# Layer 1's down projection in a two-layer trunk: seven block products in place of eight

## The chip, the cores and the metric

The kernel runs on one core of a Trainium2 chip. The metric is the device time of one execution, in microseconds (us). The engines are TensorE (PE in the profile; its weight loads are PEld), VectorE (DVE), ScalarE (ACT), GpSimd (POOL) and SyncE (SP). SP issues the loads from device memory; GpSimd's queue issues a few transfers within the core that add what they read onto what is there.

## The reference

A decoder trunk of two layers on 512 tokens of width 1024, float32 throughout. Each layer has a mixer (convolution and pooling in layer 0, chunked spatial gating in layer 1) and then a gated FFN with a causal convolution of width 3; a final RMS norm ends it. The change lies in layer 1's FFN:

```python
def gated_conv_ffn(x, w_gate, w_up, conv_w, conv_b, w_down):   # x: (1, 512, 1024)
    g = jnp.einsum('bsd,df->bsf', x, w_gate)                    # d_ff = 2816
    g = causal_dwconv3(g, conv_w) + conv_b
    up = jnp.einsum('bsd,df->bsf', x, w_up)
    return jnp.einsum('bsf,fd->bsd', jax.nn.silu(g) * up, w_down)

for layer in range(2):
    ...
    h = h + gated_conv_ffn(rms_norm(h, norm_ffn[layer]), ...)
return rms_norm(h, final_norm)
```

## The kernel before

**Splits.** Every float32 matrix is kept as two parts in the type float32r: hi is a rounded copy, lo is what is left. A product of two matrices is three matmuls (hi hi, hi lo, lo hi; lines 133 to 135). hi is made on ScalarE (`nc.scalar.activation(hi, raw, AF.Copy)`), lo on VectorE by a subtraction (`parts`, L126 to L130; `split` for activations, L247 and L249). A second way, `summed`, makes lo without VectorE: ScalarE writes the negative of the hi part, and a transfer on GpSimd's queue adds the source to it (L120, L121).

**Seven products.** Some hidden products (gate and up projections) already work on 2 x 2 blocks with seven products instead of eight (Winograd's form of Strassen's scheme), from sums of weight blocks and of activation blocks. For these `both` (gate and up) and `seven` (up alone, with plain gate products) treat a pair of FFN tiles f, f+1. An FFN tile is 128 of the 2816 hidden channels; there are 22. Products that share an accumulator share a PSUM bank: products 1, 6, 7 and 4 bank a, 5 and 3 bank e, 2 bank b.

**FFN 1.** `PARTS` says which pairs are made before which down group: (0, 2) then tiles 0 and 1; (4) then 2 to 5; (6, 8) then 6 to 9; (10, 12) then 10 to 13; (14, 16) then 14 to 17; (18, 20) then 18 to 21. So one period of the steady part is a pair by `both`, a pair by `seven`, and a down group. At the end of a pair the gate goes through the convolution (`conv`, c in a pool of two buffers) and the silu (`silu`, one s tile of 128 x 512 per FFN tile, three buffers), is multiplied by the up projection, and is split by `act` into a_hi and a_lo (four buffers each in layer 1 too).

**The down group.** For four tiles `group8` fetches four weight rows of 128 x 1024 (`raw_dn`), splits them with `parts` into whi_dn and wlo_dn, and makes eight outputs (four token tiles by two column halves) in eight PSUM banks, with the activations stationary and the weights moving. Its order is output by output, four tiles each, and a finished output is added to y on VectorE:

```python
dst = y[t][:, half * 512 : (half + 1) * 512]
nc.vector.tensor_tensor(dst, ps, dst, ALU.add)
```

The last group also squares, scales and stores the outputs.

**Order.** The framework's scheduler orders each engine's queue from the program; it may put later, ready work ahead. `inorder` (`tc.keep_in_program_order`) fixes the order among the instructions so marked. Each engine then works through its queue in order, so an instruction that waits holds up all behind it. Buffers are pools with a fixed count: four for fetched weights (`raw`, 512 KB each), six each for whi and wlo, three for weight sums (`sum`), seven PSUM banks and one more. A fetch waits until the last reader of its buffer is done, a transfer among them.

Of the kernel before, what the change touches and what calls it, by code (L numbers as in the profile page):

```python
# [30 lines left out]
def tile_trunk(ctx: ExitStack, tc: tile.TileContext, x, norm_mix, norm_ffn, final_norm,  # L31
# [3 lines left out]
    nc = tc.nc  # L35
    x = x[0]
# [4 lines left out]
    tp = ctx.enter_context(tc.tile_pool(name="tp", bufs=2))  # L41
# [3 lines left out]
    def mm_bank(name):  # L45
        return ps_mm.tile([P, 512], F32, tag="mm", name=name)
# [28 lines left out]
    inorder = tc.keep_in_program_order  # L75
# [49 lines left out]
    def parts(raw, a, b, name):  # L125
        hi = wp.tile([P, a, b], F32R, tag="whi", bufs=6, name=f"whi_{name}")  # L126
        lo = wp.tile([P, a, b], F32R, tag="wlo", bufs=6, name=f"wlo_{name}")
        nc.scalar.activation(hi, raw, AF.Copy)  # L128
        nc.vector.tensor_tensor(lo, raw, hi.bitcast(F32), ALU.subtract)  # L129
        return hi, lo  # L130
# [113 lines left out]
    def split(pool, src, name, scale=1.0, tag="a", bufs=None):  # L244
        hi = pool.tile([P, S], F32R, tag=f"{tag}hi", bufs=bufs, name=f"{name}_hi")
        lo = pool.tile([P, S], F32R, tag=f"{tag}lo", bufs=bufs, name=f"{name}_lo")
        nc.scalar.activation(hi, src, AF.Copy, scale=scale)  # L247
        if isinstance(scale, float):
            nc.vector.tensor_tensor(lo, src, hi.bitcast(F32), ALU.subtract)  # L249
# [227 lines left out]
    HALF = S // 2  # L477
# [10 lines left out]
    class Ffn:  # L488
# [5 lines left out]

        def __init__(self, layer, prm, norm, ap, sums):
            self.layer, self.prm, self.ap, self.acts = layer, prm, ap, {}
            self.norm, self.sums = norm, sums
            self.t23, self.t41 = {}, {}  # L500

        def conv(self, t, ft):
            ap, prm, n = self.ap, self.prm, f"{self.layer}_{ft}"
            c = ap.tile([P, S], F32, tag="c", bufs=2, name=f"c{n}")
            nc.scalar.activation(c, t[:, 0:S], AF.Copy, scale=prm("cf", ft))
            for i in (1, 2):
                nc.vector.scalar_tensor_tensor(c, t[:, i : S + i], prm("cf", i * NF + ft), c,  # L507
                                               op0=ALU.mult, op1=ALU.add)
# [102 lines left out]
        def multiply(self, banks, name, product, weights_):  # L611

            at = self.BANK[product]
            first = at not in banks
            if first:
                banks[at] = mm_bank(f"{name}{at}")
            ps = banks[at][:, :HALF]
            hi, lo = weights_
            for kp in range(NP):
                b_hi, b_lo = self.moving(product, kp)  # L620
                a_hi, a_lo = hi[:, kp, :], lo[:, kp, :]
                for l, r, end in ((a_hi, b_hi, False), (a_hi, b_lo, False),
                                  (a_lo, b_hi, kp == NP - 1)):
                    nc.tensor.matmul(ps, l, r, start=first, stop=end, skip_group_check=True)
                    first = False
            return ps
# [333 lines left out]
    def ffn1(norm):  # L960
        with tc.tile_pool(name="f1", bufs=1) as ap:
            def sums(kp):
                return [cp.tile([P, 2, HALF], F32R, tag=f"h{k}", name=f"t23_{k}")
                        for k in (kp, kp + NP)]

            ffn = Ffn(1, prm1, norm, ap, sums)
            acts = ffn.acts
            y = [ap.tile([P, D], F32, name=f"y{t}") for t in range(NT)]
            ssf = ap.tile([P, NT, PAD], F32, name="ssf")[:, :, :2]

            def turn_residual(t, half):
                ps = mm_bank(f"hT{t}_{half}")
                for i in range(4):
                    nc.tensor.transpose(ps[:, i * P : (i + 1) * P],
                                        h[half * 4 + i][:, t * P : (t + 1) * P], ident)
                nc.scalar.copy(y[t][:, half * 512 : (half + 1) * 512], ps)

            def before(i, j):
                if i < 2:
                    turn_residual(j, i)  # L980

            for groups, a, b in PARTS:
# [13 lines left out]

                def lhs(ft, j):
                    ts_ = slice((j // 2) * P, (j // 2 + 1) * P)
                    return acts[ft][0][:, ts_], acts[ft][1][:, ts_]

                def rhs(ft, j):
                    c = slice((j % 2) * 512, (j % 2 + 1) * 512)
                    return ch[ft][0][:, 0, c], ch[ft][1][:, 0, c]

                yf = {}

                def done(j, ps):
                    t, half = j // 2, j % 2
                    dst = y[t][:, half * 512 : (half + 1) * 512]
                    nc.vector.tensor_tensor(dst, ps, dst, ALU.add)  # L1010
# [5 lines left out]
                    yf[half] = ap.tile([P, S], F32, tag="s", bufs=3, name=f"yf{j}")  # L1016
                    nc.vector.tensor_tensor(yf[half], dst, fin[:, half * 512 : (half + 1) * 512],
                                            ALU.mult)
                    if half == 0:
                        nc.vector.tensor_scalar(ss, ss, 1.0 / D, EPS, op0=ALU.mult, op1=ALU.add)  # L1020
                        return
                    ms = ssf[:, t, 0:1]
                    nc.vector.scalar_tensor_tensor(ms, ss, 1.0 / D, ms, op0=ALU.mult, op1=ALU.add)
                    r = tp.tile([P, LINE], F32, tag="rc", name=f"rc_fin{t}")[:, :1]
                    newton(ms, 1, f"fin{t}", r)
                    nc.vector.tensor_scalar(ms, ms, 1.5, None, op0=ALU.add)
                    for c in range(2):
                        cs = slice(c * 512, (c + 1) * 512)
                        nc.vector.tensor_scalar(y[t][:, cs], yf[c], r, ms,
                                                op0=ALU.mult, op1=ALU.mult)  # L1030
# [16 lines left out]
    n = mixer0()  # L1047
# [33 lines left out]
```

## Time and profile before

| | |
|---|---|
| device time, median of 3 runs | 1006.06 us (1005.46 to 1007.25) |
| span of the profiled execution, first to last instruction | 1004.4 us |
| TensorE busy | 992.1 us, 99% of the span |
| VectorE, ScalarE, GpSimd busy | 666.0, 499.9, 94.1 us |
| layer 1's down matmuls | 528 of 128x512 |
| granted TensorE clock, mean | 0.999 |

In the profile's rows, a line such as L1010 is a line of the kernel; then come engine, operation, the tiles written and read (buffer numbers left out) and the shape. A group's row ends with its count, total and mean time. In a timeline a row starts with the start and the duration in us; in square brackets stands how long the engine was idle before it, and what ended that. A window's row gives for each engine its busy us and, in brackets, its number of instructions. TensorE's matmuls overlap, so the mean duration of one (0.39 us for 128x512) is longer than the step from one to the next.

### The profile page before, as it was taken

How to read it: one execution, taken by the hardware profiler on the slowest of the kernel's cores; microseconds unless marked ns; L12 is line 12 of the kernel's file. 1: busy time of each engine (PE TensorE's matmuls, PEld its weight loads, DVE VectorE, ACT ScalarE, POOL GpSimd, SP SyncE). 2: the span in 40 equal slices, each digit the busy share in tenths (PEclk: the TensorE clock that was granted, in tenths of full speed). 3: DMA queues.
4: the chain of work that ended last, by engine and by line, in shares of the span. 5: the costliest groups of instructions: out<-in, count | busy, mean ns of one | idle time of the engine just before them, and what ended most of it. 6: DMA issues, size and time to landing. Idle time of an engine off the chain costs nothing.

```text
span 1004.4 us, 14019 instructions
## 1 busy us (share of the span) xinstructions
PE 992.1 (99%) x5547; PEld 865.9 (86%) x5547; DVE 666.0 (66%) x993; ACT 499.9 (50%) x735; POOL 94.1 (9%) x109
## 2 busy tenths in 40 slices
PE   8999999999999999999999999999999999999997
PEld 6888888898989989899878888888989898898985
DVE  5977457968584775847833645389675857658567
ACT  6523345754553635537645434675535365353553
POOL 3032030200000000000300001212000000000000
PEclk9999999999999999999999999999999999999999
DMA  7532234554445444454433123435545345353432
GB/s 236 178 105 84 85 90 122 117 155 114 118 142 131 128 110 119 138 137 127 127 125 104 63 85 105 101 88 123 150 100 153 105 127 147 94 152 112 127 85 84
DMA packets 80749, 120.30 MB, mean 120 GB/s; under 512 B 4164, under 2 KB 53548, under 8 KB 80684
## 3 DMA queue, kind: packets, MB, share of 16 engines
q1 hardware_dynamic: 73580, 98.96, 30.9%
q0 software_dynamic: 5760, 18.88, 10.7%
q10 hardware_dynamic: 1344, 1.58, 0.5%
q8 instruction: 43, 0.70, 0.3%
q14 instruction: 22, 0.18, 0.1%
HBM read 98.42 MB, written 2.10 MB: 100 GB/s over the span
## 4 chain that ended last, share of the span: by engine, by line
PE 95%; DMA 2%; DVE 2%; ACT 1%; SPq 0%; issue 0%; POOL 0%; DVEq 0%; ACTq 0%; POOLq 0%
PE dn L133 4%; PE dn L135 4%; PE dn L134 4%; PE d L133 4%; PE d L134 4%; PE d L135 4%; PE gu L133 3%; PE g L133 3%; PE g L134 3%; PE gu L134 3%; PE gu L135 3%; PE g L135 3%; PE u L135 1%; PE oo L133 1%; PE oo L135 1%; PE u L134 1%
## 5 line engine op out<-in xcount | busy, mean ns | idle before, releaser
L507 DVE SCALAR_TENSOR_TENSOR c<-rows,prm,c 128x512 f32<-128x512 f32 x88 | 68.9, 792 | 0.3
L134 PE MATMUL d<-a_lo,whi_d 128*128 128x512 f32 x176 | 68.6, 390 | 0.0
L135 PE MATMUL d<-a_hi,wlo_d 128*128 128x512 f32 x176 | 68.5, 389 | 0.0
L133 PE MATMUL dn<-whi_dn,a_hi 128*128 128x512 f32 x176 | 68.4, 390 | 0.0
L134 PE MATMUL dn<-wlo_dn,a_hi 128*128 128x512 f32 x176 | 68.4, 390 | 0.0
L135 PE MATMUL dn<-whi_dn,a_lo 128*128 128x512 f32 x176 | 67.6, 390 | 0.0
L133 PE MATMUL d<-a_hi,whi_d 128*128 128x512 f32 x176 | 67.1, 390 | 0.0
L1010 DVE TENSOR_TENSOR y<-dn,y 128x512 f32<-128x512 f32 x48 | 32.3, 688 | 30.9 <-PE dn L135 30.7
L133 PE MATMUL g<-hgh,whi_g 128*128 128x512 f32 x128 | 50.0, 391 | 0.0
L134 PE MATMUL g<-hgl,whi_g 128*128 128x512 f32 x128 | 50.0, 391 | 0.0
L135 PE MATMUL g<-hgh,wlo_g 128*128 128x512 f32 x128 | 49.8, 389 | 0.0
L129 DVE TENSOR_TENSOR wlo_dn<-raw_dn,whi_dn 128x1024 fp32r<-128x1024 f32 x22 | 26.8, 1222 | 30.7 <-ACT whi_dn L128 30.7
L129 DVE TENSOR_TENSOR wlo_d<-raw_d,whi_d 128x1024 fp32r<-128x1024 f32 x22 | 26.8, 1221 | 30.2 <-ACT whi_d L128 30.2
L129 DVE TENSOR_TENSOR wlo_u<-raw_u,whi_u 128x1024 fp32r<-128x1024 f32 x16 | 19.6, 1223 | 34.2 <-ACT whi_u L128 34.1
L120 ACT ACTIVATE wlo_g<-raw_g 128x1024 fp32r<-128x1024 f32 x14 | 14.7, 1050 | 51.6 <-PE dn L134 51.6
L292 DVE TENSOR_TENSOR h<-d,h 128x512 f32<-128x512 f32 x48 | 32.4, 686 | 11.6 <-PE d L135 11.1
L513 ACT ACTIVATE s<-c,prm 128x512 f32<-128x512 f32 x44 | 31.6, 718 | 16.7 <-DVE c L507 16.6
L135 PEld LDWEIGHTS dn<-whi_dn,a_lo 128*128 128x128 f32 x176 | 33.0, 188 | 7.4 <-DVE a_lo L249 0.2
L134 PEld LDWEIGHTS d<-a_lo,whi_d 128*128 128x128 f32 x176 | 33.1, 188 | 7.1 <-DVE a_lo L249 0.2
L133 PEld LDWEIGHTS dn<-whi_dn,a_hi 128*128 128x128 f32 x176 | 33.1, 188 | 7.0 <-ACT a_hi L247 0.2
L133 PEld LDWEIGHTS d<-a_hi,whi_d 128*128 128x128 f32 x176 | 32.9, 188 | 7.0
L135 PEld LDWEIGHTS d<-a_hi,wlo_d 128*128 128x128 f32 x176 | 33.0, 188 | 6.8
(972 smaller groups left out, 3196.0 us busy)
## 6 DMA issues: line engine op xcount, KB each, us to landing
raw_g<-in_w_ffn_gate_dram SPq DMA_DIRECT2D x36, 512.0 KB, 4.5
raw_u<-in_w_ffn_up_dram SPq DMA_DIRECT2D x36, 512.0 KB, 3.8
raw_d<-in_w_ffn_down_dram SPq DMA_DIRECT2D x22, 512.0 KB, 3.6
raw_dn<-in_w_ffn_down_dram SPq DMA_DIRECT2D x22, 512.0 KB, 4.4
wlo_u<-raw_u POOLq DMA_DIRECT2D x18, 512.0 KB, 5.2
wlo_g<-raw_g POOLq DMA_DIRECT2D x14, 512.0 KB, 4.5
raw_oe<-in_w_out_even_dram SPq DMA_DIRECT2D x8, 512.0 KB, 3.5
raw_g<-in_w_ffn_gate_dram SPq DMA_DIRECT2D x16, 256.0 KB, 2.9
```

The source lines that it names most:

```text
L120: nc.scalar.activation(lo, raw, AF.Copy, scale=-1.0)
L129: nc.vector.tensor_tensor(lo, raw, hi.bitcast(F32), ALU.subtract)
L133: nc.tensor.matmul(ps, lhs[0], rhs[0], start=start, stop=False)
L134: nc.tensor.matmul(ps, lhs[0], rhs[1], start=False, stop=False)
L135: nc.tensor.matmul(ps, lhs[1], rhs[0], start=False, stop=stop)
L292: nc.vector.tensor_tensor(h[k], ps, h[k], ALU.add)
L507: nc.vector.scalar_tensor_tensor(c, t[:, i : S + i], prm("cf", i * NF + ft), c, op0=ALU.mult, op1=ALU.add)
L513: nc.scalar.activation(s, c, AF.Silu, bias=self.prm("bf", ft))
L1010: nc.vector.tensor_tensor(dst, ps, dst, ALU.add)
```

## The change

For tiles 2 to 17, in blocks of four tiles (a = 2, 6, 10, 14), `group8` gives way to a new function `down`. It views the block as 2 x 2: the activations as a11, a12 (first token half, first and second tile pair) and a21, a22 (second half), the weights as b11, b12, b21, b22 (pair of tiles by column half), and makes seven products, each of 2 token tiles x 2 FFN tiles x 3 matmuls of 128x512. The weight sums t1 to t4 are made on VectorE, t1, t3 and t4 in the fetched buffers themselves (b11's, b12's and b21's); four of the seven weight operands are split by `summed`, three by `parts`. The activation sums s1 and s2 are made on VectorE from the unsplit silu tiles, which are now kept in pairs of 128 x 2 x 512 (still three buffers), and every stationary operand is split by `part`. For these tiles `act` splits nothing. Each product is added to y straight from its bank while the bank goes on accumulating, two additions per product: 14 a block.

Splits of activations, their sums and the additions to y carry `inorder`, except for the first product's split. The split buffers of layer 1 are three instead of four; the conv's c comes from another pool with two buffers, in both layers; y is one tile instead of four.

```diff
+            def down(a):
+                g1, g2 = ffn.rows[a], ffn.rows[a + 2]
+                def part(src, n, order=inorder):
+                    hi = ap.tile([P, 2, HALF], F32R, tag="ahi", bufs=3, name=f"hi{n}_{a}")
+                    lo = ap.tile([P, 2, HALF], F32R, tag="alo", bufs=3, name=f"lo{n}_{a}")
+                    order(nc.scalar.activation(hi, src, AF.Copy))
+                    order(nc.vector.tensor_tensor(lo, src, hi.bitcast(F32), ALU.subtract))
+                    stat[n] = hi, lo
...
+                def multiply(product, at, half, c):
+                    (hi, lo), (whi, wlo) = stat[product], mov[product]
+                    for i in range(2):
+                        first = (at, i) not in banks
+                        ...
+                        for k in range(2):
+                            for l, r, end in ((hi, whi, False), (hi, wlo, False),
+                                              (lo, whi, k == 1)):
+                                nc.tensor.matmul(ps, l[:, k, ts_], r[:, k, :], start=first,
+                                                 stop=end, skip_group_check=True)
+                                first = False
+                        dst = y[2 * half + i][:, c * 512 : (c + 1) * 512]
+                        inorder(nc.vector.tensor_tensor(dst, ps, dst, ALU.add))
+                mov[1] = parts(*b11)
+                part(a11, 1, free)
+                mov[2] = parts(*b21)
+                t1, t4, t3 = b11[0], b21[0], b12[0]
+                minus(t1, b12[0], b11[0], free)
+                t2 = ap.tile([P, 2, 512], F32, tag="sum", bufs=3, name=f"t2_{a}")
+                minus(t2, b22[0], t1, free)
+                mov[6] = summed(t2, 2, 512, f"{name}_t2")
+                mov[5] = summed(t1, 2, 512, f"{name}_t1")
+                minus(t3, b22[0], b12[0], free)
+                mov[7] = summed(t3, 2, 512, f"{name}_t3")
+                minus(t4, b21[0], t2, free)
+                ...
+                part(a12, 2)
+                inorder(nc.vector.tensor_tensor(s1, a21, a22, ALU.add))
+                minus(s2, s1, a11)
+                part(s2, 6)
+                multiply(1, "a", 0, 0)
+                part(s1, 5)
+                minus(s1, a11, a21)
+                multiply(2, "b", 0, 0)
+                part(s1, 7)
+                mov[3] = parts(*b22)
+                multiply(6, "a", 0, 1)
+                minus(s2, a12, s2)
+                part(s2, 3)
+                multiply(5, "e", 1, 1)
+                part(a22, 4)
+                mov[4] = summed(t4, 2, 512, f"{name}_t4")
+                multiply(7, "a", 1, 1)
+                multiply(3, "e", 0, 1)
+                multiply(4, "a", 1, 0)
...
             for groups, a, b in PARTS:
                 for f in groups:
                     ffn.hidden(f, before=before)
                 last = b == NF
+                if a in (2, 6, 10, 14):
+                    down(a)
+                    continue
...
         def conv(self, t, ft):
-            c = ap.tile([P, S], F32, tag="c", bufs=2, name=f"c{n}")
+            c = tp.tile([P, S], F32, tag="sq", name=f"c{n}")
...
         def silu(self, c, ft):
-            s = self.ap.tile([P, S], F32, tag="s", bufs=3, name=f"s{self.layer}_{ft}")
+            f = ft - ft % 2
+            if f not in self.rows:
+                self.rows[f] = self.ap.tile([P, 2, S], F32, tag="s", bufs=3, ...)
+            s = self.rows[f][:, ft % 2, :]
...
         def act(self, ft, s):
-            self.acts[ft] = split(self.ap, s, f"a{self.layer}_{ft}", tag="a", bufs=4)
+            if ft not in self.kept:
+                self.acts[ft] = split(self.ap, s, f"a{self.layer}_{ft}", tag="a",
+                                      bufs=4 if self.layer == 0 else 3)
```

More of the change, by code (lines that the diff above doesn't have):

```diff
@@ L488, in tile_trunk, with __init__ @@
     class Ffn:
-        def __init__(self, layer, prm, norm, ap, sums):
+        def __init__(self, layer, prm, norm, ap, sums, kept=()):
             self.layer, self.prm, self.ap, self.acts = layer, prm, ap, {}
@@ L511, in silu @@
         def silu(self, c, ft):
-            s = self.ap.tile([P, S], F32, tag="s", bufs=3, name=f"s{self.layer}_{ft}")
+            f = ft - ft % 2
+            if f not in self.rows:
+                self.rows[f] = self.ap.tile([P, 2, S], F32, tag="s", bufs=3,
+                                            name=f"s{self.layer}_{f}")
+            s = self.rows[f][:, ft % 2, :]
             nc.scalar.activation(s, c, AF.Silu, bias=self.prm("bf", ft))
@@ L964, in sums @@
                         for k in (kp, kp + NP)]
-            ffn = Ffn(1, prm1, norm, ap, sums)
+            ffn = Ffn(1, prm1, norm, ap, sums, range(2, 18))
             acts = ffn.acts
-            y = [ap.tile([P, D], F32, name=f"y{t}") for t in range(NT)]
+            y_all = ap.tile([P, NT, D], F32, name="y")
+            y = [y_all[:, t, :] for t in range(NT)]
             ssf = ap.tile([P, NT, PAD], F32, name="ssf")[:, :, :2]
@@ L980, in before, with block, minus, free @@
                     turn_residual(j, i)
+            def down(a):
+                g1, g2 = ffn.rows[a], ffn.rows[a + 2]
+                name = f"dn{a}"
+                def part(src, n, order=inorder):
[4 more added lines that the diff above has]
+                    stat[n] = hi, lo
+                def block(r, c):
+                    rows = slice((a + 2 * r) * P, (a + 2 * r + 2) * P)
+                    return fetch(w_ffn_down[1][rows, c * 512 : (c + 1) * 512]
+                                 .rearrange("(k p) c -> p k c", p=P), 2, 512, f"{name}_{r}{c}")
+                def minus(dst, x, y_, order=inorder):
+                    order(nc.vector.tensor_tensor(dst, x, y_, ALU.subtract))
+                def free(ins):
+                    return ins
+                a11, a21 = g1[:, :, :HALF], g1[:, :, HALF:]
+                a12, a22 = g2[:, :, :HALF], g2[:, :, HALF:]
+                b11, b21, b12, b22 = block(0, 0), block(1, 0), block(0, 1), block(1, 1)
+                mov, stat, banks = {}, {}, {}
+                def multiply(product, at, half, c):
+                    (hi, lo), (whi, wlo) = stat[product], mov[product]
+                    for i in range(2):
+                        first = (at, i) not in banks
+                        if first:
+                            banks[at, i] = mm_bank(f"{name}{at}{i}")
+                        ps = banks[at, i]
+                        ts_ = slice(i * P, (i + 1) * P)
+                        for k in range(2):
[18 more added lines that the diff above has]
+                minus(t4, b21[0], t2, free)
+                s1, s2 = (tp.tile([P, 2, HALF], F32, tag="rstd", name=f"as{i}_{a}")
+                          for i in range(2))
+                part(a12, 2)
[17 more added lines that the diff above has]
+                multiply(4, "a", 1, 0)
@@ L1015, in done @@
                     nc.scalar.activation(sq, dst, AF.Square, accum_out=ss)
-                    yf[half] = ap.tile([P, S], F32, tag="s", bufs=3, name=f"yf{j}")
+                    if half == 0:
+                        yf["pair"] = ap.tile([P, 2, S], F32, tag="s", bufs=3, name=f"yf{j}")
+                    yf[half] = yf["pair"][:, half, :]
                     nc.vector.tensor_tensor(yf[half], dst, fin[:, half * 512 : (half + 1) * 512],
```

1 line of the change is left out of this document (added).

## The prediction

> **What bounds the kernel now.** I read the page first, for the busy shares and for the chain that ended last.
>
> ```profile
> span 1004.4 us, 14019 instructions
> ...
> PE 992.1 (99%) x5547; PEld 865.9 (86%) x5547; DVE 666.0 (66%) x993; ACT 499.9 (50%) x735; POOL 94.1 (9%) x109
> ...
> PE 95%; DMA 2%; DVE 2%; ACT 1%; SPq 0%; issue 0%; POOL 0%; DVEq 0%; ACTq 0%; POOLq 0%
> ```
>
> TensorE is busy for 99% of the span and carries 95% of the chain; VectorE and ScalarE stand at 66% and 50%. The next view is the list of what TensorE waited for (total, times, longest).
>
> ```profile
> PE wst L851 <- POOL ws L844: 1.6, 1, 1.6
> PE clock L56 <- DVE idle L53: 1.3, 1, 1.3
> PE xt_ps L357 <- DMA xt<-in_x_dram: 1.1, 1, 1.1
> PE z L134 <- DVE hgl L370: 1.0, 2, 0.8
> ```
>
> That is the whole list: 5 us, none of it in layer 1's FFN. So while the changed part runs, time goes only where TensorE's queue goes: a matmul taken away is time gained, and any wait put in front of one is time lost. The windows view gives one period of layer 1's FFN (two hidden pairs and one down group of four tiles), and a down group by itself; after the engine's busy us stands its instruction count.
>
> ```profile
> core 0: us, PE busy (x) PEld busy (x) DVE busy (x) ACT busy (x) POOL busy (x), PEclk, DMA share, GB/s
> 786.00:808.00 22.00, 22.00 (x101) 18.25 (x100) 14.26 (x23) 5.03 (x6) 0.86 (x1) 1.00 0.26 72
> 786.00:849.10 63.10, 63.10 (x397) 57.27 (x396) 42.02 (x63) 30.77 (x45) 2.57 (x3) 1.00 0.47 126
> ```
> ```profile
> 786.00:808.00 22.00, 21.52 (x95) 17.43 (x93) 5.18 (x8) 1.00 0.26 72
> ```
>
> TensorE fills the 63.1 us. VectorE has 42.0 us of work in it, ScalarE 30.8 us. Inside the group VectorE works 14.3 us, of which the tile view gives 5.2 us to the sums into y; the other 9.1 us are the next pair's weights. A down matmul takes 21.52/95 = 0.227 us.
>
> **What goes.** A block of four tiles had 8 outputs x 4 tiles x 3 = 96 matmuls; seven products of 2 row halves x 2 tiles x 3 make 84. That is 12 fewer in each of four blocks: 48 x 0.227 = **-10.9 us**. The queues of the built program show these 48 and no other change of TensorE's count, and up to the first block all queues hold the same work as before, so I cost layer 0 (the conv scratch in another pool, the paired silu tiles) at nothing.
>
> **What comes.** The step from start to start is the price on VectorE and ScalarE, since the last 0.09 us of each instruction overlaps the next.
>
> ```profile
> 778.07 1.23 DVE L129 TENSOR_TENSOR wlo_dn<-raw_dn,whi_dn 128x1024 fp32r<-128x1024 f32 x1 [6.25 <-ACT whi_dn L128]
> ...
> 780.64 2.20 DVE L507 SCALAR_TENSOR_TENSOR c<-rows,prm,c 128x512 f32<-128x512 f32 x3
> 782.75 0.42 DVE L769 TENSOR_TENSOR kept<-u_8e,kept 128x256 f32<-128x256 f32 x1
> ...
> 788.02 0.69 DVE L634 TENSOR_TENSOR wlo_a<-raw_u,whi_a 128x512 fp32r<-128x512 f32 x1
> 788.62 0.69 DVE L653 TENSOR_TENSOR s12g<-raw_g,raw_g 128x512 f32<-128x512 f32 x1
> 789.22 0.69 DVE L249 TENSOR_TENSOR a_lo<-s,a_hi 128x512 fp32r<-128x512 f32 x1
> ...
> 791.63 1.28 DVE L1010 TENSOR_TENSOR y<-dn,y 128x512 f32<-128x512 f32 x2
> 792.83 1.22 DVE L634 TENSOR_TENSOR wlo_s12g<-s12g,whi_s12g 128x1024 fp32r<-128x1024 f32 x1
> 793.96 0.69 DVE L1010 TENSOR_TENSOR y<-dn,y 128x512 f32<-128x512 f32 x1
> ...
> 808.28 1.23 DVE L634 TENSOR_TENSOR wlo_s34g<-s34g,whi_s34g 128x1024 fp32r<-128x1024 f32 x1
> 809.42 1.22 DVE L634 TENSOR_TENSOR wlo_s12u<-s12u,whi_s12u 128x1024 fp32r<-128x1024 f32 x1
> ```
> ```profile
> 788.14 0.63 ACT L247 ACTIVATE a_hi<-s 128x512 fp32r<-128x512 f32 x1 [1.44 <-DVE s L793]
> ...
> 809.10 1.04 ACT L122 ACTIVATE whi_u<-raw_u 128x1024 fp32r<-128x1024 f32 x1
> 810.05 1.04 ACT L120 ACTIVATE wlo_u<-raw_u 128x1024 fp32r<-128x1024 f32 x1
> ```
>
> A 128x512 pass on VectorE takes 0.60 us (788.02 to 788.62; a y addition the same, two in 791.63 to 792.83), a 128x1024 pass 1.13 (792.83 to 793.96). On ScalarE a 128x1024 pass takes 0.95 (809.10 to 810.05) and a 128x512 split 0.63, of which I count 0.52 to the next start, by the same overlap. A block drops 4 activation splits, 4 weight splits and 8 y additions on VectorE (12 x 0.60 + 4 x 1.13 = 11.7 us) and gains 7 splits, 4 activation sums and 14 y additions of 512 with 3 weight splits and 4 weight sums of 1024 (25 x 0.60 + 7 x 1.13 = 22.9 us): +11.2 us. ScalarE drops 5.9 us and gains 14.1: +8.2. SP's four fetches keep their size. GpSimd's queue gains four accumulating transfers of 512 KB.
>
> On average this fits: 53.2 us on VectorE in a period of 63.1 - 2.7 = 60.4. In the place it does not. While the 84 matmuls run (19.1 us), VectorE has 25 x 0.60 + 1.13 = 16.1 us of the block's own work, kept in program order, and the 9.1 us of the next pair's weights, 25.2 in all. Some 6 us must run after the block, when TensorE is already in the next pair. And the products are chained: each sum waits for the sum before it, each reuse of bank a or e for its y additions. I price the waits with t = 0 at the block's first matmul.
>
> *Product 2* needs the split of the tile finished last. Before, the group also began while that tile was being made:
>
> ```profile
> 785.55 0.40 PE L133 MATMUL dn<-whi_dn,a_hi 128*128 128x512 f32 x1
> ```
>
> The rows above have its hi half at 788.14 + 0.63, 3.2 us after this start, and its lo half at 789.22 + 0.69, 4.4 us after. Product 1 covers 12 x 0.227 = 2.7. Then hi costs 0.5 and lo, two matmuls later, another 0.6; there is slightly less in VectorE's queue now, but two passes of 0.95 stand before the hi split on ScalarE. I take 1.0, bounds 0.5 to 1.2.
>
> *Products 6 and 5* need, from the arrival of lo 2: s1 (0.60), the split of b22 that stands between (1.13), s2 (0.69), and two ScalarE splits (0.52 + 0.62), 3.6 us; TensorE has ten matmuls of product 2 left, 2.3. Wait 1.25, bounds 1.2 to 1.3.
>
> *Product 7* writes bank a, so product 6 must have been added to y. In VectorE's queue those additions stand behind the lo half of product 7, whose hi half stands on ScalarE behind the split of the next pair's up weights, and that split waits for a transfer. Their buffer is b12's, held until t3's accumulating transfer has landed. The trace's landing times (min/median/max) for such a transfer, and for the fetch of up weights:
>
> ```profile
> DMA to landing us min/median/max: 4.5/5.2/7.6
> ```
> ```profile
> DMA to landing us min/median/max: 2.9/4.6/7.6
> ```
>
> t3's transfer is issued some 1.9 us after the block's start, two ScalarE passes in. By medians: 1.9 + 5.2 + 4.6, then 0.52 + 0.62 on ScalarE and 0.60 + 0.69 on VectorE: 14.1. TensorE arrives at 2.7 + 1.0 + 2.7 + 1.25 + 2.7 + 2.7 and four short matmuls, 13.6. Wait 0.5 by medians, 6 by the longest of both (7.6). Here the fetch follows another fetch while t4's transfer is in flight, so I take 2.5.
>
> [...]
>
> *The next pair* begins with g_10a in this view of the chain (start, us, matmuls), and at u_10b it needs the lo part of its second up weights, a transfer too:
>
> ```profile
> 784.28 1.44 PE u_8e L624 x12
> ...
> 807.52 1.43 PE g_10a L624 x12
> ...
> 819.21 1.44 PE u_10b L624 x12
> ```
> ```profile
> 811.39 0.85 POOL L121 DMA_DIRECT2D wlo_u<-raw_u  x1 [3.88 <-DVE s L730]
> ```
>
> That is 11.7 us of cover, and the transfer left at 811.39, 3.9 after the start, because VectorE then had only 808.28 and 809.42 left to do. Now it still has two passes of 1.13 and five of 0.60 ahead of the up sums, 5.3 us, then three ScalarE passes of 0.95: the transfer leaves 8.2 after, lands by the median at 13.4, by the longest at 15.8. Loss 1.7 to 4.1, partly in small waits on the way; beside fetches I take 3.0.
>
> *The pair before the next block* (the one with plain gate products) gets four weight sums into VectorE's queue. VectorE idled 6.25 us before 778.07, which covers most of these 4.5 us; the addition at 782.75 ended 1.1 us before the last product that reuses its bank (784.28 in the chain above). I take 0.9, bounds 0 to 2.3.
>
> Together 1.0 + 1.25 + 2.5 + 3.0 + 0.9 = 8.65 a block, **+34.6 us** for four. Two terms occur once; for the second, the view of VectorE near the end shows its closing work on one pair of outputs, from one final scaling to the next.
>
> ```profile
> 989.15 1.00 DVE L1029 TENSOR_SCALAR y<-yf,rc_fin,ssf 128x512 f32<-128x512 f32 x2
> ...
> 994.41 1.00 DVE L1029 TENSOR_SCALAR y<-yf,rc_fin,ssf 128x512 f32<-128x512 f32 x2
> ```
>
> In the first block the split of the next pair's gate weights stands ahead of hi 6 on ScalarE, so that product 5 waits for t1's transfer and a fetch: 0.3 + 5.2 + 4.6 + 1.7 = 11.8, where the other blocks start it at 5.4 + 2.25 = 7.7: **+4**, bounds 0 to 4. And with three split buffers instead of four, the last group takes tiles 18 and 19 for all eight outputs first; its outputs then end every 6 matmuls (1.4 us) instead of 12, faster than VectorE's closing work on them (994.41 - 989.15 = 5.3 us for two), so the last y addition starts late: **+3**, bounds 0 to 3.5.
>
> Sum: -10.9 + 34.6 + 4 + 3 = +30.7 us. The span of 1004.4 us has 1.7 us around it to the median of 1006.06; I carry that over: **1037 us**. With all low bounds a block loses 3.9: -10.9 + 15.6, 1011; with the high ones 14.9: -10.9 + 59.6 + 7.5, 1062.
>
> **The rivals.** *The cover holds (faster).* VectorE's and ScalarE's shares speak for it: if the next pair's splits slip in between without holding the chain, and transfers land at their shortest, only the 48 matmuls count: 995 us. It decides in favour when the waits stay under 2.7 us a block. Against it, the dependence of products 5 to 7 needs no contention at all and costs 2.2 by itself. Chance 0.05; another 0.02 that gain and waits cancel.
>
> *The transfers become the bound (slower still).* Four more accumulating transfers per block on the same queues, each holding a fetch buffer: if they land at 7.6 as the longest row does, product 7 waits 6 and the next pair 4.1, 13.25 a block: -10.9 + 53 + 7, 1055. Chance 0.2.
>
> *TensorE's clock falls in the gaps.* The granted clock is 1.00 in the windows above, but there TensorE has no gap; the longest of the list is 1.6 us. If a gap of 2.5 to 4 us halves the clock for as long as one product, each costs 2.7 us: one or two a block, 11 to 22 us on top, 1048 to 1059. [...] Chance 0.1.
>
> **How the numbers follow.** My forecast has 0.63. The range, 1011 to 1062, is that of the terms' bounds and takes in both slower rivals; the faster one lies outside. About 2 us (0.2%) is what can be told from no change here: faster 0.05, same 0.02, slower 0.93.
>
> **What would show it.** In the profile after: 480 dn matmuls instead of 528; waits of TensorE on VectorE and ScalarE within the dn products, a period of about 69 us, product 7's on a y addition and the next pair's on wlo_u; VectorE busy some 53 us a period. Wrong if the list of TensorE's waits stays as short as above, if the granted clock drops, or if the waits sit on the weight sums instead.

## The result and the profile after

The changed kernel takes **1047.74 us** (median of 4 runs, 1045.5 to 1049.27) against 1005.76 (1004.25 to 1007.25): the ratio is 1.0414, 95% interval 1.0394 to 1.0434. It is slower by 42 us; the forecast was 1037, in a range of 1011 to 1062. The page of the profiled execution:

```profile
span 1047.3 us, 14102 instructions
...
PE 1000.1 (95%) x5499; PEld 866.5 (83%) x5499; DVE 709.4 (68%) x1057; ACT 534.0 (51%) x775; POOL 106.7 (10%) x125
...
PE 74%; DMA 10%; ACT 5%; DVE 5%; issue 4%; SPq 0%; DVEq 0%; ACTq 0%; POOLq 0%
```

TensorE has the 48 instructions less, and its share has fallen from 99% to 95%; its part of the chain from 95% to 74%, where transfers, ScalarE and VectorE now stand. The list of what TensorE waited for had four lines before, the latest of them at 507 us, ahead of layer 1's FFN. Now its head reads (total us, times, longest):

```profile
PE dn2e L1028 <- ACT hi L997: 2.8, 1, 2.8
PE dn6a L1028 <- DVE y L1032: 2.7, 1, 2.7
PE dn14a L1028 <- DVE y L1032: 2.7, 1, 2.7
PE dn10a L1028 <- DVE y L1032: 2.6, 1, 2.6
PE u_6b L631 <- DMA wlo_u<-raw_u: 2.4, 1, 2.4
PE dn2b L1028 <- ACT hi L997: 1.9, 1, 1.9
PE u_16e L631 <- DVE kept L776: 1.8, 1, 1.8
PE u_12e L631 <- DVE kept L776: 1.8, 1, 1.8
PE u_18a L631 <- ACT kept L689: 1.5, 1, 1.5
PE u_14a L631 <- ACT kept L689: 1.5, 1, 1.5
PE u_18b L631 <- DMA wlo_u<-raw_u: 1.4, 1, 1.4
PE u_14b L631 <- DMA wlo_u<-raw_u: 1.3, 1, 1.3
```

The waits at dn are inside the blocks; u_6b, u_14a, u_14b, u_18a and u_18b are in the pair behind a block; u_12e and u_16e in the plain pair ahead of one. The windows view from product 7 of one block to product 7 of the next (columns as in the prediction):

```profile
810.92:884.20 73.28, 64.56 (x385) 56.32 (x385) 53.59 (x79) 39.49 (x55) 6.02 (x7) 0.98 0.53 137
884.20:957.84 73.64, 65.36 (x384) 58.04 (x385) 53.67 (x79) 39.51 (x55) 6.02 (x7) 0.95 0.53 136
```

A period is now 73.3 and 73.6 us where it was 63.1, with 53.6 us of VectorE's work. The last thing to read is in the columns behind: the granted clock is 0.98 and 0.95. Windows of 3.41 us around two equal waits, those at dn10a (2.88 us from the start of the last short matmul before it, 0.12 of them its own step) and dn14a (2.96 us), show how it falls:

```profile
879.40:882.81 3.41, 2.19 (x12) 1.72 (x10) 0.61 (x2) 1.15 (x2) 0.00 (x0) 1.00 1.04 355
882.81:886.22 3.41, 2.02 (x9) 1.71 (x10) 3.41 (x6) 0.86 (x2) 0.00 (x0) 1.00 0.35 106
886.22:889.63 3.41, 3.41 (x21) 2.99 (x20) 3.41 (x7) 0.67 (x2) 0.00 (x0) 1.00 0.00 0
951.06:954.47 3.41, 3.41 (x16) 2.81 (x16) 2.43 (x4) 0.00 (x0) 0.00 (x0) 1.00 0.99 228
954.47:957.89 3.42, 0.74 (x6) 0.53 (x5) 1.49 (x3) 1.15 (x2) 0.00 (x0) 1.00 0.89 300
957.89:961.30 3.41, 3.41 (x8) 2.66 (x9) 3.41 (x7) 1.15 (x2) 0.00 (x0) 0.51 0.01 4
```

The second wait lies in one window, with TensorE busy for 0.74 of 3.42 us, and the next window has half the clock (0.51). The first wait lies across two windows, each busy for over 2 us, and the clock stays at 1.00. Seven such windows at half clock lie in layer 1's FFN of this execution.

Summed over TensorE's records from 685 us on (each step from one start to the next beyond 0.227 us for 512 columns, 0.12 for 256), the span's 42.9 us are: waits 41.9 in place of 0.7, +41.2, steps at half clock +10.8, 48 matmuls -10.9, from the start of the last matmul to the end 11.1 us in place of 7.8, +3.4, and an earlier start of this part, -1.6.

### The profile page after: what moved, and what is told of

The parts are those of the page before. It is cut to its first block, busy times and chain, and to the rows that moved or that the text cites. A ratio compares the mean times of both kernels' runs of the same rounds, so it can differ in the third digit from the quotient of the medians.

```text
span 1047.3 us, 14102 instructions
## 1 busy us (share of the span) xinstructions
PE 1000.1 (95%) x5499; PEld 866.5 (83%) x5499; DVE 709.4 (68%) x1057; ACT 534.0 (51%) x775; POOL 106.7 (10%) x125
## 4 chain that ended last, share of the span: by engine, by line
PE 74%; DMA 10%; ACT 5%; DVE 5%; issue 4%; SPq 0%; DVEq 0%; ACTq 0%; POOLq 0%
DMA wlo_u<-raw_u 4%; PE d L133 4%; PE d L134 4%; PE d L135 4%; PE gu L133 3%; PE gu L134 3%; PE gu L135 3%; DMA raw_g<-in_w_ffn_gate_dram 2%; PE g L133 2%; PE g L134 2%; PE g L135 2%; PE v L133 1%; PE u L135 1%; PE oo L135 1%; PE u L133 1%
## 5 line engine op out<-in xcount | busy, mean ns | idle before, releaser
L121 POOL DMA_DIRECT2D wlo_u<-raw_u x18 | 15.4, 858 | 250.3 <-ACT wlo_u L120 188.1
L189 POOL TENSOR_TENSOR ssq_f<-ssq_f,sq_f 128x512 f32<-128x512 f32 x12 | 16.3, 1358 | 180.0 <-ACT sq_f L188 145.1
L121 POOL DMA_DIRECT2D wlo_g<-raw_g x14 | 12.2, 873 | 219.5 <-DVE h L292 80.1
L175 ACT ACTIVATE hgh<-h,prm 128x512 fp32r<-128x512 f32 x24 | 17.3, 720 | 32.0 <-DVE h L292 32.0
L129 DVE TENSOR_TENSOR wlo_g<-raw_g,whi_g 128x1024 fp32r<-128x1024 f32 x20 | 24.4, 1219 | 13.6 <-ACT whi_g L128 13.6
L640 ACT ACTIVATE whi_s12u<-s12u 128x1024 fp32r<-128x1024 f32 x10 | 10.6, 1061 | 43.6 <-PE d L134 32.2
L176 DVE SCALAR_TENSOR_TENSOR hgl<-h,prm,hgh 128x512 fp32r<-128x512 f32 x24 | 22.1, 922 | 15.0 <-ACT hgh L175 14.9
L128 ACT ACTIVATE whi_d<-raw_d 128x1024 fp32r<-128x1024 f32 x22 | 23.2, 1055 | 17.7 <-PE g L134 14.0
```

The costliest lines, as they stand in the source:

```text
L121: nc.gpsimd.dma_start(lo, raw, accum_op=ALU.add)
L175: nc.scalar.activation(hg[k][0], h[k], AF.Copy, scale=g)
L176: nc.vector.scalar_tensor_tensor(hg[k][1], h[k], g, hg[k][0].bitcast(F32), op0=ALU.mult, op1=ALU.subtract)
L189: nc.gpsimd.tensor_tensor(self.ssq, self.ssq, sq, ALU.add)
```

## The experiments

The theory (A): every block has a chain of its own over ScalarE, VectorE and a transfer that holds a fetch buffer; its waits make TensorE idle, and the idle time makes the clock fall. The rivals are VectorE's load alone (B), the transfers alone (C), and in single runs others, named with their prices. Medians below stand beside 1005.0 to 1005.5 for the kernel before on the same chip.

**t3's lo part on VectorE (e1_p7).**

```diff
-                mov[7] = summed(t3, 2, 512, f"{name}_t3")
+                mov[7] = parts(t3, 2, 512, f"{name}_t3")
```

> Product 7's weight operand (the sum t3) gets its lo part from VectorE, as the plain blocks do, in place of the accumulating transfer; one line changed. Theory A (product 7's wait is a chain: t3's transfer holds the fetch buffer, so the next pair's up weights come late, their split stands at ScalarE's head, and hi 7, lo 7 and the y additions stand behind it): the waits of 2.7 us at dn6a, dn10a and dn14a go (-8.9 us in steps), the two falls of the clock behind them too (about -3 us), and the pass of 1.13 us that VectorE gains per block costs at most 1 us a block: 1036 to 1039 us. Theory B (VectorE's load is the cause): four more passes of 1.13 us, no wait goes: 1049 to 1053. Theory C (transfers are slow in general): one of four transfers less, the waits at wlo_u shrink as well, product 7's stays: 1043 to 1046.

Measured: 1039.74 us (1037.97 to 1045.34), ratio 1.0352 (1.0322 to 1.0383). Beside the transfer, the line takes one ScalarE pass of 0.95 us out of a block and puts one of 1.13 on VectorE. In the change this is what product 7 of block 10 waited for, in the timelines of ScalarE, VectorE and TensorE:

```profile
881.58 0.63 ACT L640 ACTIVATE whi_a<-raw_u 128x512 fp32r<-128x512 f32 x1 [4.14 <-DMA raw_u<-in_w_ffn_up_dram]
882.11 0.61 ACT L997 ACTIVATE hi<-as 128x512 fp32r<-128x512 f32 x1
```
```profile
882.76 0.69 DVE L998 TENSOR_TENSOR lo<-as,hi 128x512 fp32r<-128x512 f32 x1 [2.80 <-ACT hi L997]
883.37 1.28 DVE L1032 TENSOR_TENSOR y<-dn10a,y 128x512 f32<-128x512 f32 x2
```
```profile
884.20 0.47 PE L1028 MATMUL dn10a<-whi_dn_t,hi 128*128 128x512 f32 x1 [2.60 <-DVE y L1032]
```

ScalarE stood 4.14 us before the next pair's up weights, hi 7 started right behind them, VectorE stood 2.80 us for that hi, and only then came lo 7 and the additions that free bank a. The link from t3's transfer to the fetch stands in SP's timeline, first of the change, then of this run:

```profile
875.35 0.37 SPq L110 DMA_DIRECT2D raw_u<-in_w_ffn_up_dram  x1
```
```profile
870.96 0.50 SPq L110 DMA_DIRECT2D raw_u<-in_w_ffn_up_dram  x1
```

In the change t3's transfer started at 869.92 on GpSimd's queue, and the fetch of the up weights went out 5.4 us later. Counted from the first matmul of u_12e ahead of the block (866.36 and 864.80) it went out after 9.0 us there and after 6.2 here, and ScalarE now stands 0.73 us before these weights in place of 4.14. With the one transfer gone the wait list has no dn6a, dn10a or dn14a any more; waits in sum fall from 41.9 to 33.3 us, steps at half clock from 10.8 to 8.4. That is theory A's place and nearly its price (1036 to 1039); B and C are out for product 7. In the first block, which never waited there, product 5's wait grew to 4.1 us.

**Without the additions of products 1, 6, 5 and 7 (e2_noadd).**

```diff
+                        if product in (1, 6, 5, 7):
+                            continue
                         dst = y[2 * half + i][:, c * 512 : (c + 1) * 512]
                         inorder(nc.vector.tensor_tensor(dst, ps, dst, ALU.add))
```

> Leaves out of the result the additions to y of products 1, 6, 5 and 7 (8 of the 14 of a block, 4.8 us of VectorE per block), and with them the wait for bank a's reuse. Theory A: product 7 still waits for hi 7 and lo 7, which stand behind the up weights' split on ScalarE; about 1.4 us of its 2.9 us step stays, now with ScalarE as what ended it, the next pair's waits on ScalarE and VectorE shrink by 1 to 2 us a block: 1032 to 1038 us. Theory B (VectorE's load): 19 us of work gone, the waits of products 2, 5 and 7 and of the next pair all go but for the transfer's: 1015 to 1022. Theory D (the additions in fixed order hold bank a, nothing else): product 7's wait under 0.3 us, the others as before: 1033 to 1036, with the difference to A visible in the wait list only.

Measured: 1028.22 us, ratio 1.0229 (1.0211 to 1.0247); faster than A said, slower than B. The wait list:

```profile
PE dn2a L1028 <- ACT hi L997: 3.7, 1, 3.7
PE dn10a L1028 <- ACT hi L997: 3.0, 2, 2.6
PE dn14a L1028 <- ACT hi L997: 3.0, 2, 2.5
PE dn6a L1028 <- ACT hi L997: 2.9, 2, 2.5
...
PE u_14a L631 <- ACT kept L689: 1.0, 1, 1.0
```

Without the additions product 7 waits all the same, 2.5 us, and now for hi 7 itself: bank a's reuse was not the cause but the end of the chain (D is out). In the first block product 6 waits 3.7 us for hi 6, behind the split of the next pair's gate weights, for which ScalarE stands 2.78 us; that the waits inside the blocks would all go, as B had it, is wrong. What was gained beyond A's price came from elsewhere: all waits at wlo_u are gone, and of those at kept behind a block one of 1.0 is left. No transfer was touched here; with 4.8 us less on VectorE per block no wait at wlo_u is left. So the next pair's loss is VectorE's backlog, as the prediction had it, and B is right there.

**One block alone (e3_only10, e10_only2).** Only the set of tiles and the list of blocks change, to (10,) or (2,):

```diff
-            ffn = Ffn(1, prm1, norm, ap, sums, range(2, 18))
+            ffn = Ffn(1, prm1, norm, ap, sums, range(10, 14))
-                if a in (2, 6, 10, 14):
+                if a in (10,):
```

> Only the block of tiles 10 to 13 goes by seven products, the rest as before the change (in the layout after it, with three split buffers). Theory A (each block's waits come from its own chain): one block costs its 10.5 us of waits (pair before 2.0, products 0.8, 1.35 and 2.9, next pair 3.4) less 2.7 us of matmuls, the tail 3.4 us, the clock 1 to 3: 1017 to 1021 us. Theory E (backlog carried from block to block): a single block costs under 5 us of waits: 1008 to 1013.

> Only the first block (tiles 2 to 5) goes by seven products, the rest as before the change. By the steps seen in the profile after: product 2 2.3 us, product 5 3.2, the next pair 2.7 at wlo_u and 0.7 at its gate, no pair before it; less 2.7 us of matmuls, plus the tail 3.4 and two falls of the clock, 3: 1005.2 + 12.6 = 1018 us, no more than the block of tiles 10 to 13 alone (1018.04). If the first block costs 4 us more than the others, as the prediction had it: 1020 to 1022.

Measured: 1018.04 us (ratio 1.0129, 1.0114 to 1.0145) and 1018.31 (1.0136, 1.0119 to 1.0152). One block costs 12.6 and 13.3 us, 3.4 of them the closing part, which comes once: 9.2 to 9.9 times 4, plus 3.4, is 40 to 43, and the four cost 42. Theory E (under 5 us of waits for a single block) is out, and the first block is no dearer than another. A little is carried all the same: alone, block 10 and its pairs lose 10.5 us in steps at full clock, among four 12.0, and the pair ahead of it makes the difference (0.8 alone, 2.55 among four). The first block's waits are others:

```profile
PE dn2e L1028 <- ACT hi L997: 2.7, 1, 2.7
PE u_6b L631 <- DMA wlo_u<-raw_u: 2.4, 1, 2.4
PE dn2b L1028 <- ACT hi L997: 1.9, 1, 1.9
```

Product 5 waits here, as the prediction said, and product 7 then doesn't.

**Four split buffers (e4_a4).**

```diff
-                                      bufs=4 if self.layer == 0 else 3)
+                                      bufs=4)
-   ... tag="ahi", bufs=3, ... tag="alo", bufs=3, ...
+   ... tag="ahi", bufs=4, ... tag="alo", bufs=4, ...
```

> Layer 1's split buffers are four again instead of three, all else as in the change. Theory A: only the tail gets better, as the last group returns to outputs that end every 12 matmuls: 3 to 3.5 us less, 1044 to 1045 us; the waits in the blocks stay. Theory F (too few split buffers hold the products up): the waits of products 5 and 7 shrink by 1 us or more each: under 1040.

Measured: 1054.62 us, ratio 1.0483 (1.0465 to 1.05): slower than the change, which neither theory had. The closing part did shrink, from 11.1 to 7.8 us, and the waits are nearly the same, 42.9 us in place of 41.9. But thirteen windows of 3.41 us at half clock lie in this part (the expectation of e9_fill_a4 counts twelve), some side by side, the mean granted clock from 685 to 1013 us is 0.93 in place of 0.96, and steps at half clock cost 17.7 us in place of 10.8; another 1.5 us came before this part. That the clock took the gain is borne out by the second of the next two runs; why it falls oftener here, and whether the same way in the three runs without a trace (all four took 1052.17 to 1055.06), stays open.

**Filler matmuls in the idle time (e5_fill, e9_fill_a4).**

```diff
+    def fill(n, name):
+        ps, still = aux_bank(f"fill_{name}"), ident.bitcast(BF16)
+        for i in range(n):
+            inorder(nc.tensor.matmul(ps[:, :256], still[:, :P], still, start=i == 0,
+                                     stop=i == n - 1))
...
+                    n = ({2: 16, 6: 36, 7: 14} if a == 2 else {2: 8, 7: 14}).get(product, 0)
+                    if n:
+                        fill(n, f"{name}_{product}")
```

> 260 small bf16 matmuls (128x256, the identity's bits on both sides, into the spare bank, read by nobody) stand where TensorE waited: before products 2, 6 and 7 of the first block, 2 and 7 of the others, and in layer 1's pairs before the matmuls that wait for kept and wlo_u. They take the place of idle time and nothing else. Theory A (the granted clock falls because TensorE idles, 10.8 us of the loss): no window at half clock is left or one at most, and the time falls by 7 to 11 us though TensorE has 260 instructions more: 1036 to 1041 us. Theory G (the clock falls for another reason, such as load, or the halved clock only fills time in which TensorE would have waited): 1047 to 1053, with the falls still there or with longer waits in their place.

> The run with the filler matmuls, with four split buffers in layer 1 instead of three. The run with four buffers alone was slower, its closing part 3.4 us shorter but its clock at half in twelve windows instead of seven. Theory A (the four buffers gain their 3.4 us, and the clock's falls, which follow from where the idle stretches lie, took them away): with the idle time filled the gain shows, 1038 to 1040 us against 1042.65. Theory F2 (four buffers cost something else in the blocks): 1043 us or more.

Measured: 1042.65 us (ratio 1.0367, 1.0347 to 1.0387) and, with four split buffers, 1040.04 (1.0348, 1.0332 to 1.0363). Beside the fillers of the diff, 9 or 14 each stand in layer 1's pairs before products that waited. The wait list of the first run:

```profile
PE dn2a L1041 <- DVE y L1045: 2.7, 1, 2.7
PE dn14a L1041 <- DVE y L1045: 1.7, 1, 1.7
PE dn10a L1041 <- DVE y L1045: 1.6, 1, 1.6
```

One window at half clock is left in each, behind the 2.7 us at dn2a (2.5 in the second run); from 685 to 1013 us the mean granted clock is 0.99 in both, in place of 0.96, and steps at half clock fall from 10.8 to 1.6 and 1.2 us, though TensorE has 260 instructions more. The whole gain is 5 and not 7 to 11 us, because the fillers cost a little more than the waiting that they replaced: the profiled span is 4.6 us shorter, made of -24.5 (waits, 41.9 to 17.4), -9.2 (clock), +1.4 (this part starts later) and so 27.7 for 260 fillers, 0.107 each. So in this kernel the clock's falls come with TensorE's idle time: with 17.4 us of waits in place of 41.9, one fall of seven is left. And with the other falls gone, four buffers are 2.6 us faster than three, near the 3.4 first expected, though the two runs' ranges (1040.29 to 1044.41 and 1038.78 to 1040.32) just touch.

**All four lo parts on VectorE, or on GpSimd (e6_parts, e7_gp).** Either `parts` in place of `summed` for t2, t1, t3 and t4, or the same with the subtraction on GpSimd:

```diff
+    def pooled_lo(raw, a, b, name):
+        ...
+        nc.scalar.activation(hi, raw, AF.Copy)
+        nc.gpsimd.tensor_tensor(lo, raw, hi.bitcast(F32), ALU.subtract)
```

> All four lo parts of t1, t3, t2 and t4 come from VectorE in place of accumulating transfers: 16 transfers less, 16 passes of 1.13 us more on VectorE (18 us), 16 ScalarE passes of 0.95 us less (15 us). Theory A: product 7's waits go, as with t3 alone, but products 2 and 5 wait up to 1.1 us longer each, as VectorE's passes stand before their splits: 1038 to 1043 us, no better than the run with t3 alone. Theory B (VectorE's load decides): 1055 to 1066. Theory C (transfers and the fetches behind them decide): 1022 to 1032.

> The same four lo parts come from a subtraction on GpSimd, which is idle there: 16 transfers less, VectorE's work as in the change, 16 ScalarE passes less. Theory A (the block's chain over ScalarE and VectorE, held up by transfers): products 2, 5 and 7 wait under 1 us each from the second block on, the next pair's waits at kept and wlo_u stay (VectorE's and ScalarE's backlog, a transfer of the hidden pair itself): 1026 to 1034 us. Theory B (VectorE's load alone): 1043 to 1048. A subtraction on GpSimd that slows VectorE beside it would put it above 1040 too, with VectorE's passes longer than 0.60 and 1.13 us.

Measured: 1045.77 us (ratio 1.0412, 1.0396 to 1.0427) and 1064.22 (1.0591, 1.0576 to 1.0607). On VectorE the 16 transfers' waits come back as VectorE's, more of them than A had:

```profile
PE u_12e L631 <- DVE kept L776: 2.8, 1, 2.8
PE u_16e L631 <- DVE kept L776: 2.8, 1, 2.8
...
PE dn14e L1028 <- ACT hi L997: 1.8, 1, 1.8
...
PE dn10e L1028 <- ACT hi L997: 1.8, 1, 1.8
PE dn10b L1028 <- ACT hi L997: 1.7, 1, 1.7
```

Product 7 no longer waits, but products 2 and 5 wait 1.7 and 1.8 us in blocks 6 and 10 where the change's list had 0.3 and 1.0, and the plain pair waits 2.8 ahead of blocks 10 and 14, where it was 1.8. Taking t3's transfer alone away gained 8 us; taking the other three too gave 6 of them back. On GpSimd it is worse than all expectations but the last clause; its timeline and VectorE's:

```profile
869.62 3.29 POOL L129 TENSOR_TENSOR wlo_dn_t<-t,whi_dn_t 128x1024 fp32r<-128x1024 f32 x1 [11.42 <-ACT whi_dn_t L128]
872.87 3.32 POOL L129 TENSOR_TENSOR wlo_dn_t<-raw_dn,whi_dn_t 128x1024 fp32r<-128x1024 f32 x1
```
```profile
869.43 1.22 DVE L136 TENSOR_TENSOR wlo_dn<-raw_dn,whi_dn 128x1024 fp32r<-128x1024 f32 x1
870.68 3.31 DVE L1014 TENSOR_TENSOR raw_dn<-raw_dn,t 128x1024 f32<-128x1024 f32 x1
873.92 4.28 DVE L515 SCALAR_TENSOR_TENSOR c<-rows,prm,c 128x512 f32<-128x512 f32 x3
```

GpSimd's 16 passes took 2.4 to 3.3 us each for what VectorE does in 1.13, and VectorE's own pass of 1.13, begun at 870.68 beside it, took 3.31 us: it ended at 873.99, 1.1 after GpSimd's first pass did (869.62 + 3.29 = 872.91). The next group, three passes, took 4.28 in place of the 2.20 of before. Of GpSimd's 3.29 us, 2.26 lie behind the end of the VectorE pass beside which it began (869.43 to 870.65), near the 2.4 of its shortest; whether the rest is waiting is not shown. Beside the engine that was to relieve it VectorE is slower, 3.24 us from start to start in place of 1.13 in the pass begun at 870.68, and with it the plain pair comes late: it waits 5.9 us. Why the two slow each other is not shown.

**The block one pair later (e8_late, e11_late_parts).** The block of one period is called after the first pair of the next; t1, t2 and t3 by `parts`, four split buffers; t4's lo on GpSimd in the first run, by its transfer in the second.

```diff
-                for f in groups:
+                for i, f in enumerate(groups):
                     ffn.hidden(f, before=before)
+                    if i == 0 and a - 4 in (2, 6, 10, 14):
+                        down(a - 4)
```

> The block's work stands one pair later in the program (after the first pair of the next period), the lo parts of t1, t2 and t3 come from VectorE, that of t4 from GpSimd, and the split buffers are four. Theory A: the operands lie ready when the block starts, no transfer holds a fetch buffer, the tail is 3.4 us shorter; what stays are the waits that VectorE's and ScalarE's backlog makes (about 2 us at products 2 and 5 and in the plain pair): 1018 to 1026 us, still slower than before the change. Theory H (the waits come from the chain of seven products itself, wherever it stands): 1032 to 1040.

> As the run with the block one pair later, but the lo part of t4 comes by its transfer again and not from GpSimd (those of t1, t2, t3 from VectorE; four split buffers). If GpSimd's subtraction slows VectorE beside it, as the run with all four on GpSimd showed (a pass of 1.13 us took 3.2), this gives back 2 to 3 us in three blocks: 1028 to 1033 us, still slower than before. If the transfer of t4 holds a fetch buffer that the plain pair needs, as t3's did: 1037 or more.

Measured: 1037.17 us (ratio 1.0318, 1.0303 to 1.0334) and 1032.5 (1.0278, 1.0248 to 1.0308). The first missed A's 1018 to 1026 and lies in H's 1032 to 1040 (the chain waits wherever it stands): eight windows at half clock stay (8.9 us; the mean granted clock of the execution is 0.986, with 0.985 in the change), GpSimd has one pass per block, and the last block waits 6.7 us for its first split. The second is the fastest variant that computes all four blocks in full, and still 27 us slower than before:

```profile
PE dn14a L1028 <- ACT hi L997: 8.1, 1, 8.1
PE dn2b L1028 <- DVE lo L998: 3.1, 1, 3.1
PE u_8e L631 <- DVE kept L776: 1.9, 1, 1.9
PE dn10b L1028 <- DVE lo L998: 1.8, 1, 1.8
...
PE dn10e L1028 <- ACT hi L997: 1.8, 1, 1.8
```

The 8.1 us are the last block's: its first split stands on ScalarE behind the splits of tiles 18 and 19, the pair just ahead of it now. Moved, the block still waits 1.8 us at product 2 and 1.8 at product 5 in blocks 6 and 10, as H has it. But e6_parts, with the block in its old place and the same passes on VectorE, has 1.7 and 1.8 there, so place and passes are not told apart. Product 7's wait and those in the pair by `both` are gone, against H; the plain pair, which now stands right behind the block, waits 1.7 to 1.9. To break even, waits and clock together would have to stay under 2.7 us a block.

## Why the prediction was right, and where it was off

*What bounds the kernel, and that waits decide.* Right: 48 matmuls less, 53.6 us on VectorE a period (53 was said), and the time went to waits at the places named. The period came out at 73.5 instead of 69.

*Product 2.* Said 1.0 (0.5 to 1.2). In blocks 6 and 10 the steps lose 0.9, in block 14 nothing, in the first 2.1.

*Products 6 and 5.* Said 1.25; 1.2, 1.2 and 0.7 in blocks 6, 10 and 14.

*Product 7.* Said 2.5 between 0.5 and 6; 2.9, 2.8 and 2.8. The chain was the one described, link by link, and e1_p7 and e2_noadd show it; 2.5 itself was a choice within a wide range. The sentence that product 6's additions hold the bank is true of what came last, but they are not its cause.

*The next pair.* Said 3.0 (1.7 to 4.1); 3.8, 3.9, 4.5 and 4.6, above the upper bound twice. The step that failed counted the transfer of wlo_u and let the pair's other waits into its scatter: the trace has 1.4 to 1.8 us at u_10a, u_14a and u_18a for kept, and 1.0 at the gate sums (0.7 at g_a and 0.4 at g_e), ahead of 1.3 to 1.7 at wlo_u. The landing time was well taken:

```profile
wlo_u<-raw_u POOLq DMA_DIRECT2D x18, 512.0 KB, 5.3
...
wlo_dn_t<-raw_dn POOLq DMA_DIRECT2D x12, 512.0 KB, 5.4
```

5.3 and 5.4 us by the median for 512 KB (last column), where the prediction had 5.2.

*The pair before.* Said 0.9 (0 to 2.3); 1.35, 2.55 and 2.15 in the three blocks that have one, none in the first. The step that failed let VectorE's idle 6.25 us cover most of the 4.5 us of weight sums. In the change VectorE idles as long, but until the last of the block's weights has come:

```profile
859.11 1.23 DVE L1007 TENSOR_TENSOR t<-raw_dn,raw_dn 128x1024 f32<-128x1024 f32 x1 [6.96 <-DMA raw_dn<-in_w_ffn_down_dram]
```

Three of the four sums run only then, back to back with a split, and push back the convolution and the addition for which u_12e waits.

*The first block.* Said 4 on top of the others. Product 5's wait came (3.3), but it took product 7's place instead of being added, and with no plain pair's wait before it this block costs 9.1 us in all, the others 10.3, 12.0 and 10.2. e10_only2 shows it as no dearer: the time that this term added was not there.

*The tail.* Said 3; 3.4 (11.1 in place of 7.8), and back to 7.8 in e4_a4, e9_fill_a4 and e11_late_parts with four buffers.

*Layer 0 at nothing.* Right within the scatter: the last matmul of the pair before the first block starts at 720.7 us, 1.6 earlier than before, and at 721.5 to 722.1 in e1_p7, e4_a4 and e5_fill, against 722.3 before.

Over all, the waits added 41.2 us where the terms with the first block's had 38.6. That is 2.6 of the 12.2 us by which the span lies above the forecast's (1004.4 + 30.7 = 1035.1); the clock is 10.8, the tail 0.4, the earlier start -1.6. That the waits' sum came so near is partly luck: the pairs before and behind the blocks cost some 7 us more than their terms, products 5, 6 and 7 with the first block's term some 4 less.

*The rivals.* "TensorE's clock falls in the gaps" had 0.1 and came true, on top of the forecast as it said: seven falls in four blocks at 1.5 us each, 10.8 us where one or two a block at 2.7 had been priced at 11 to 22, and e5_fill takes 9.2 of it back. It was set low because the profile before has no such gap to judge by; but the forecast itself put waits of 2.5 and 3 us into every block, and by its own condition those were the gaps that count. Of its price, no run shows a fall that lasts one product and costs 2.7 us; in the change's profile each lasted 3.41 us, behind 1.8 to 2.7 us of idle time in the 3.41 us before. A drop of the granted clock stood among the prediction's own signs of being wrong, and in this it was: the forecast has the waits and no clock, and the time lies in the range because the range was wide enough to take in this rival too. "The transfers become the bound" did not: those on GpSimd's queue landed at 5.3 and 5.4 us by the median. "The cover holds" did not come true either: the waits took some 10 us a block, not under 2.7.

## What to carry to other kernels

TensorE was 99% busy before; there a saved matmul was worth 0.23 us, 48 of them 10.9, and the dependences put into its stream cost 41.2 us of waits. So price the chain from operand to operand on the slower engines before counting matmuls. An instruction that waits for a transfer, put ahead of a critical one on the same in-order queue, makes that transfer part of the chain, as where ScalarE stood 4.14 us before the split of the up weights, with hi 7 behind it; find it by following idle time back from TensorE over VectorE to ScalarE. The gaps cost twice here, 41.2 us as gaps and 10.8 by the clock, and a variant that only moves them can win or lose several us: e4_a4 has 42.9 us of waits in place of 41.9, and 17.7 by the clock.

## What the runs showed of the hardware

Between 690 us and the last matmul of the change's profile the granted clock is 1.00 but for seven stretches at 0.50. Each of them lasts 3.41 us, and their starts (725.82 the first, 985.24 the last) lie whole multiples of 3.413 us apart, to 0.01 us; the windows here are cut on that grid. In the 3.41 us before them, from 722.41, 729.24, 807.74, 906.73, 937.45, 954.52 and 981.82 us on, TensorE was busy for 1.47, 1.00, 0.68, 1.60, 1.63, 0.73 and 1.36 us, so idle for 1.8 to 2.7. In the 85 other windows that lie there at full clock, with the window after each, it was busy for 1.85 us or more (1.85 from 759.96 on), and the clock was 1.00 in the window after every one. What happens between 1.63 and 1.85 us is not shown, and the busy time is from the profile's modelled ends of matmuls. The wait at dn10a, 2.88 us across two windows, is among those with no fall behind it; the one at dn14a, 2.96 us and in one window, has one.

While TensorE waited for product 7, transfers filled 1.04 and 0.89 of the 16 engines' time (windows 879.40 and 954.47 above, at 355 and 300 GB/s) where the page's mean is 123 GB/s. Ahead of the first of these windows and in it, three weight fetches go out (875.35, 875.81 and 880.34).
